# S5 in a four-layer trunk: the order of TensorE's work around the GELU's transposes

## The chip, the cores and the metric

The kernel runs on one core of a Trainium2 chip. The metric is the device time of one execution in microseconds (us). "Before" is the kernel as it was, "after" the one with the change. The engines are called as in the profile: PE is TensorE (PEld its weight loads), DVE is VectorE, ACT is ScalarE, POOL is GpSimd and SP is SyncE, which issues most transfers here.

## What is computed

A trunk of four layers on 512 positions of 1024 channels. Each layer is `x += mixer(rmsnorm(x))`, then `x += ffn(rmsnorm(x))`. The mixers are S5, gated linear attention, differential attention and S5 again. The change touches only the two S5 mixers, which are cut here to what matters:

```python
for u_c in chunks(u):                      # 64 positions, 64 groups of 16 channels, 64 states each
    bu_re, bu_im = u_c @ bb_re, u_c @ bb_im
    s = associative_scan(complex_diagonal, (a, bu))     # s[t] = a s[t-1] + bu[t]
    s += p * carry
    y_c = s_re @ c_re - s_im @ c_im
y = y + d_skip * h
z = gelu(y)
a, b = split(z @ w_glu)
x = x + a * sigmoid(b)
```

## The kernel before, in words

Each S5 mixer is a pipeline over eight blocks of 128 channels (`s5_pipe`, L1542). Step kk of its loop (L1668) works on several blocks at once, each at another stage. For block kk there are, in order:

- `up` (L1571): PE turns the normed input into channels by time (tile "up"), ACT copies it to `room`.
- `products` (L1582): 8 matmuls (in the profile two instructions each, since they are of full fp32) of the block with its input operators `inm` into the PSUM tile "V".
- `states` (L1590), `scan` (L1600) and `turn` (L1604): DVE multiplies V by cosines and sines (`cs`), scans twice along time and turns the result back into four products `prods`, one per k.
- `outputs` (L1617), one step later: 20 matmuls into the tile "y". For each of four groups b there is one on the "map" (the part of y that comes from the inputs of the same piece, L1622) and four on the states (`prods`, L1624). ACT then takes the GELU (L1626).
- `turned` (L1638): PE transposes the GELU's result into the tile "zp", and ACT rounds it to the high half of `zT` (L1643). `rest` (L1645): DVE subtracts to get the low half (L1647).
- `glu` (L1649), one step later still: 12 matmuls of the GLU's gate half (four pieces of the positions, three for high and low halves: L448, L449, L450) into four accumulators that stay open over all blocks. Its weights come as `whl`, a high half cast by ACT (`high`, L420) and a low half made by DVE (`low`, L428).

The first mixer (`s5_first`) also computes its operators on the way: powers (Q on DVE, X on DVE and POOL, L1239 to L1241), the operators' transposes ("xps", L1386, copied to `inm` by ACT, L1409), rows for the map ("rps", L1352, sent through DRAM back to SBUF by L1368 and L1377), and the phases of `cs`: two PE groups ("rough", L1199, and "angle", L1207), a clip on DVE (L1212) and sines on ACT. These are hung into the loop by named hooks, such as `beside` (L1908). The second mixer (`s5_second`) has them computed earlier and spilled to DRAM; its operators come back by transfers from SP (L1964, L1971).

The order on every engine is the order in which this code is written: `hand_all` (L376) switches the scheduler off inside the loop. Every engine takes its queue strictly in order. The PSUM tiles "up", "y", "zp", "xps", "cps" and "rps" share two buffers (`tp`, L395), so each waits for the reader of the one before the last; V has two banks, the accumulators and the phases' tiles share four.

Before, the loop of a step on PE reads: outputs of block kk-1, operators' transposes (first mixer), `up` of block kk+2, the GELU's transposes of block kk-1, products of block kk+1, then the GLU of block kk-2.

Of the kernel before, what the change touches and what calls it, by code (L numbers as in the profile page):

```python
# [22 lines left out]
P = 128  # L23
D = 1024
SEQ = 512
NT = SEQ // P
KT = D // P
# [313 lines left out]
class Trunk:  # L341
# [1200 lines left out]
    def s5_pipe(self, L, hu, zT, natural, room, get, before=None, hooks=None, steps=None, left=None):  # L1542
# [6 lines left out]
        mm = nc.tensor.matmul  # L1549
# [67 lines left out]
        def outputs(kk):  # L1617

            U, om, mop, q = room[kk % 4], get(kk, "out"), get(kk, "map"), hold[kk % 2][1]
            yb = self.tp("y")  # L1620
            for b in range(4):
                mm(yb[:, b], U[:, bs(b)], mop[:, bs(b)], start=True, stop=False)  # L1622
                for j in range(4):
                    mm(yb[:, b], q[:, j, b], om[:, j // 2, bs(b)], start=False, stop=j == 3)  # L1624
            z = room[4 + kk % 2].rearrange("p (t n) -> p t n", t=4)
            nc.scalar.activation(  # L1626
                z.rearrange("p t (g h) -> p g t h", h=16),
                yb[:].rearrange("p b (g t h) -> p (b g) t h", t=4, h=16), AF.Gelu_apprx_tanh,
            )
# [16 lines left out]
            d = dst(kk)  # L1646
            v.tensor_tensor(d[1], src(kk), d[0].bitcast(F32), op=ALU.subtract)  # L1647

        def glu(kk):  # L1649
            if not accs:  # L1650
                accs.extend(self.acc() for _ in range(NT))
            hl = hls[kk // 2]
            for t in range(NT):
                ts = slice(t * P, (t + 1) * P)
                self.mm3(
                    accs[t][:], zT[:, 0, kk, ts], zT[:, 1, kk, ts], hl[:, 0, kk % 2], hl[:, 1, kk % 2],
                    kk == 0, kk == KT - 1,
                )

        if hooks:  # L1660
            hook = lambda name, kk: hooks[name](kk) if name in hooks else None
            early = hooks.get("early", ())
            self.hand_all()
            if left:
                for kk in range(4):
                    up_first(kk)
            before(up, products)
            for kk in range(10):  # L1668
                if kk % 2 == 0 and kk:
                    hls[kk // 2 - 1] = self.high(stage[kk // 2 - 1], 2, 512)  # L1670
                hook("first", kk)
                if kk < 8:
                    states(kk)
                if kk == 7:
                    rest(5)
                hook("ahead of low", kk)
                if kk % 2 == 0 and kk:
                    self.low(hls[kk // 2 - 1], stage[kk // 2 - 1])
                hook("behind states", kk)
                if 1 <= kk < 9:  # L1680
                    outputs(kk - 1)
                hook("operators", kk)
                late = left and kk + 2 < 4
                if kk + 2 < 8 and not late:
                    up(kk + 2)
                hook("ahead of zp", kk)
                if 1 <= kk < 9:
                    turned(kk - 1)
                hook("behind zp", kk)
                if kk == 8:  # L1690
                    glu(6)
                if kk + 1 < 8:
                    products(kk + 1)
                hook("behind products", kk)
                if kk < 8:
                    scan(kk, 0)
                    scan(kk, 1)
                    hook("behind scans", kk)
                    for k in range(4):
                        turn(kk, k)  # L1700
                if late:
                    up(kk + 2)
                hook("ahead of rest", kk)
                if kk in early:
                    rest(kk - 1)
                hook("beside", kk)
                if 1 <= kk < 9 and kk != 6 and kk not in early:
                    rest(kk - 1)
                if kk % 2 == 0 and kk < 8:
                    stage[kk // 2] = self.staged(self.wb_src(wg, kk, D), 2, 512)  # L1710
                if kk >= 2 and kk != 8:
                    glu(kk - 2)
                hook("last", kk)
            self.hand()
            return accs
# [33 lines left out]
    def s5_first(self, ctx):  # L1749
# [5 lines left out]
        with self.tc.tile_pool(name="s5_0", bufs=1) as p:  # L1755
# [75 lines left out]
            def out_pads(kk):  # L1831
                self.s5_out_pads(oms[kk % 2], Q[kk // 2][0], slice(4 * (kk % 2), 4 * (kk % 2) + 4))
# [75 lines left out]
            def beside(kk):  # L1908
# [9 lines left out]
                if kk % 2 and kk < 7:  # L1918
                    Q[h + 1][2]()
                    Q[h + 1][3]()  # L1920
                    out_pads(kk + 1)
                if kk == 1:
                    phases((4, "clip"), (5, "clip"))

# [1 line left out]
            hooks = {  # L1926
                "first": first, "early": (2, 4), "ahead of low": ahead_of_low, "ahead of rest": ahead_of_rest, "operators": operators, "behind states": behind_states, "ahead of zp": ahead_of_zp, "behind zp": behind_zp,
                "behind products": behind_products, "behind scans": behind_scans, "beside": beside,
            }
            accs = self.s5_pipe(0, hu, zT, True, room, get, before, hooks)  # L1930
        self.x = self.xp.tile([P, NT, D], F32, tag="x", name="x")
# [875 lines left out]
```

## Time and profile before

| | us |
|---|---|
| median of three runs | 2251.64 |
| lowest and highest run | 2249.75, 2251.73 |
| the profiled execution | 2249.67 |
| span of its profile | 2248.0 |
| PE busy, share of the span | 2174.6, 97% |
| DVE busy, share of the span | 1635.6, 73% |
| first S5 pipeline, until its last GELU's transposes | 139.35 from the start |
| second S5 pipeline, from its first products to its last GELU's transposes | 1745.73 to 1829.43 |

The profile is that of one execution. A row of the timeline gives the start, the length, the engine, the line, the operation, output and inputs, the sizes and how many, and in brackets how long the engine had stood idle and what ended that. Lengths of matmuls are modelled: the next one starts before the length is over, so costs are better read from start to start. A row of the stretches gives the bounds, the length, then the busy time (and number of instructions) of PE, weight loads, DVE, ACT and POOL, the granted PE clock (1.00 is full), the share of the DMA engines and GB/s.

### The profile page before, as it was taken

What the parts mean: (1) busy time and instruction counts of PE and PEld (TensorE: products, weight loads), DVE (VectorE), ACT (ScalarE), POOL (GpSimd) and SP (SyncE); (2) the same over time, 40 slices, a digit from 0 to 9 for tenths busy, and PEclk for the clock granted to TensorE, in tenths of its full rate; (3) what the DMA queues carried; (4) which work ended last, traced back from release to release, by engine and by line L of the source; (5) the groups of instructions that cost most, each with busy time, mean ns of one, the idle gap of its engine ahead of it and who ended that gap; (6) DMA issues with size and microseconds to landing.
All of it is one profiled execution on the core that took longest, in us unless ns stands there. A gap on an engine that the chain in (4) does not pass through costs nothing.

```text
span 2248.0 us, 38450 instructions
## 1 busy us (share of the span) xinstructions
PE 2174.6 (97%) x15415; PEld 1971.6 (88%) x15415; DVE 1635.6 (73%) x2495; ACT 1138.7 (51%) x1827; POOL 341.1 (15%) x447
## 2 busy tenths in 40 slices
PE   6999999999999999999999999999999899999998
PEld 5888979989988899999888888999998888989997
DVE  9955868786878598776745676967766965957675
ACT  8534635444655365564435776644544234635443
POOL 5401141431211010100002221110000001101000
PEclk9999999999999999999999999999999999999999
DMA  4356666674863666765337465985631546766622
GB/s 90 65 171 169 164 159 174 174 184 131 206 152 95 168 168 191 179 171 139 104 128 160 96 148 141 243 207 136 184 94 47 160 141 159 196 160 164 165 76 75
DMA packets 309180, 333.62 MB, mean 148 GB/s; under 512 B 70477, under 2 KB 253033, under 8 KB 308874
## 3 DMA queue, kind: packets, MB, share of 16 engines
q1 hardware_dynamic: 238970, 238.93, 35.0%
q0 software_dynamic: 70032, 92.23, 21.9%
q8 instruction: 121, 1.98, 0.4%
q14 instruction: 57, 0.47, 0.1%
HBM read 297.16 MB, written 18.75 MB: 141 GB/s over the span
## 4 chain that ended last, share of the span: by engine, by line
PE 81%; DVE 8%; ACT 4%; issue 3%; DMA 1%; SPq 1%; POOL 0%; DVEq 0%; POOLq 0%; ACTq 0%
PE a L594 20%; PE acc L448 11%; PE acc L450 11%; PE acc L449 11%; PE c L594 10%; PE d L594 5%; PE y L1624 2%; DVE whl L428 2%; ACT whl L420 1%; PE op L2590 1%; PE V L1588 1%; PE s L2557 1%; PE tp L117 1%; PE acc L2645 1%; DMA wst<-in_ffn_w_down_dram 1%
## 5 line engine op out<-in xcount | busy, mean ns | idle before, releaser
L428 DVE TENSOR_TENSOR whl<-wst,whl 128x1024 fp32r<-128x1024 f32 x260 | 316.8, 1223 | 224.5 <-ACT whl L420 223.4
L420 ACT CAST whl<-wst 128x1024 fp32r<-128x1024 f32 x260 | 272.1, 1051 | 256.3 <-PE acc L450 164.6
L594 PE MATMUL a<-side,whl 128*128 128x256 f32 x3240 | 392.5, 277 | 6.7 <-DVE whl L428 6.3
L594 PEld LDWEIGHTS a<-side,whl 128*128 128x128 f32 x3240 | 379.0, 188 | 9.0 <-DVE whl L428 7.3
L448 PE MATMUL acc<-whl,act 128*128 128x512 f32 x704 | 276.2, 393 | 0.9 <-DVE g L768 0.9
L449 PE MATMUL acc<-whl,act 128*128 128x512 f32 x704 | 274.9, 391 | 0.0
L450 PE MATMUL acc<-whl,act 128*128 128x512 f32 x704 | 274.8, 390 | 0.0
L594 PE MATMUL c<-side,whl 128*128 128x256 f32 x2160 | 261.3, 277 | 3.5 <-DVE whl L428 3.5
L594 PEld LDWEIGHTS c<-side,whl 128*128 128x128 f32 x2160 | 253.0, 188 | 4.4 <-DVE whl L428 4.3
L428 DVE TENSOR_TENSOR whl<-slot,whl 128x1024 fp32r<-128x1024 f32 x105 | 127.6, 1221 | 60.7 <-ACT whl L420 60.7
L448 PEld LDWEIGHTS acc<-whl,act 128*128 128x128 f32 x704 | 132.4, 188 | 29.6 <-DVE g L768 1.5
L450 PEld LDWEIGHTS acc<-whl,act 128*128 128x128 f32 x704 | 132.4, 188 | 27.7
L449 PEld LDWEIGHTS acc<-whl,act 128*128 128x128 f32 x704 | 132.5, 188 | 26.4 <-issue 0.2
L420 ACT CAST whl<-slot 128x1024 fp32r<-128x1024 f32 x105 | 109.9, 1053 | 86.3 <-PE acc L450 46.3
L594 PE MATMUL d<-sides,whl 128*128 128x256 f32 x1080 | 132.3, 278 | 2.5 <-ACT whl L420 2.5
L594 PE MATMUL a<-sides,whl 128*128 128x256 f32 x1080 | 132.6, 279 | 1.6 <-DVE whl L428 1.2
L594 PEld LDWEIGHTS d<-sides,whl 128*128 128x128 f32 x1080 | 127.9, 188 | 3.3 <-ACT whl L420 3.3
L594 PEld LDWEIGHTS a<-sides,whl 128*128 128x128 f32 x1080 | 128.2, 188 | 2.8 <-DVE whl L428 1.4
L428 DVE TENSOR_TENSOR whl<-halves,whl 128x1024 fp32r<-128x1024 f32 x87 | 105.8, 1221 | 30.7 <-ACT whl L420 30.4
L420 ACT CAST whl<-halves 128x1024 fp32r<-128x1024 f32 x87 | 91.0, 1051 | 70.6 <-DVE halves L817 26.0
L759 POOL DMA_DIRECT2D wst<-in_ffn_w_gate_up_dram x44 | 57.2, 1299 | 448.7 <-DMA wst<-in_ffn_w_gate_up_dram 144.5
L865 ACT CAST act<-r 128x512 fp32r<-128x512 f32 (+1 forms) x110 | 66.1, 642 | 106.0 <-DVE r L846 85.4
(496 smaller groups left out, 4068.6 us busy)
## 6 DMA issues: line engine op xcount, KB each, us to landing
wst<-in_ffn_w_gate_up_dram SPq DMA_DIRECT2D x88, 512.0 KB, 4.6
wst<-in_ffn_w_down_dram SPq DMA_DIRECT2D x88, 512.0 KB, 4.6
slot<-in_ffn_w_gate_up_dram SPq DMA_DIRECT2D x69, 512.0 KB, 6.2
wst<-in_ffn_w_gate_up_dram POOLq DMA_DIRECT2D x44, 512.0 KB, 6.1
halves<-in_ffn_w_gate_up_dram SPq DMA_DIRECT2D x42, 512.0 KB, 6.5
wst<-in_s_w_glu_dram SPq DMA_DIRECT2D x32, 512.0 KB, 4.9
wst<-in_diff_w_qkv_dram SPq DMA_DIRECT2D x24, 512.0 KB, 4.4
slot<-in_ffn_w_gate_up_dram POOLq DMA_DIRECT2D x18, 512.0 KB, 9.2
```

The source lines that it names most:

```text
L117: tr.nc.tensor.transpose(p[:, j], h[:, j * P : (j + 1) * P], tr.ident[:])
L420: self.last["high"] = self.nc.scalar.copy(hl[:, 0], w[:])
L428: self.last["low"] = self.nc.vector.tensor_tensor(hl[:, 1], w[:], hl[:, 0].bitcast(F32), op=ALU.subtract)
L448: mm(out, lh, rh, start=first, stop=False)
L449: mm(out, lh, rl, start=False, stop=False)
L450: self.last["mm"] = mm(out, ll, rh, start=False, stop=last)
L594: mm(o, *two, start=first and not (j or k or n), stop=k == 3 and n == 2, skip_group_check=True,)
L759: nc.gpsimd.dma_start(w[:], left.quarter(*plus, b), accum_op=ALU.add)
L865: self.last["act high"] = nc.scalar.copy(dst[:, 0, j], src[:, j])
L1588: mm(V[kk][z][:, bs(b)], inm[:, z, bs(b)], U[:, bs(b)], start=True, stop=True)
L1624: mm(yb[:, b], q[:, j, b], om[:, j // 2, bs(b)], start=False, stop=j == 3)
L2557: nc.tensor.matmul(ss[m][:], qs[:, m, ts], ks[:, m, z], start=z == 0, stop=z == 1)
```

## The change

Four moves, and nothing is added to or taken from the work:

1. The products of block kk+1 stand ahead of the GELU's transposes of block kk-1 instead of behind them (both mixers).
2. A first piece of the GLU of block kk-2 stands ahead of those products: two matmuls at steps 3 to 5 of the first mixer, none there in the second, four at steps 6 to 8 of both. To let it run early, the GLU's 12 matmuls of blocks 1 to 6 come in another order: first those of two positions' pieces that use only the weights' high half.
3. The outputs of block 0 are no longer group by group. In the first mixer come the 16 matmuls on the states, then the four on the map; in the second the four on the map, then the 16.
4. In step 1 of the first mixer the low half of block 0 (`rest`) stands ahead of the clips of phases 4 and 5 on DVE.

```diff
             yb = self.tp("y")
-            for b in range(4):
+            if kk == 0:
+                by_map = [(b, U[:, bs(b)], mop[:, bs(b)]) for b in range(4)]
+                by_state = [(b, q[:, j, b], om[:, j // 2, bs(b)]) for b in range(4) for j in range(4)]
+                whole = by_map + by_state if left else by_state + by_map
+                for n, (b, x, y) in enumerate(whole):
+                    mm(yb[:, b], x, y, start=n == 0, stop=n == 19, skip_group_check=True)
+            for b in range(4 if kk else 0):
                 mm(yb[:, b], U[:, bs(b)], mop[:, bs(b)], start=True, stop=False)
...
-        def glu(kk):
+        order = {}
+
+        def glu(kk, n=12):
+
             if not accs:
                 accs.extend(self.acc() for _ in range(NT))
+            if kk not in order:
+                split = [(t, n) for t in range(2) for n in (0, 2)] + [(0, 1), (1, 1)] if 0 < kk < KT - 1 else []
+                order[kk] = split + [(t, n) for t in range(len(split) // 3, NT) for n in range(3)]
             hl = hls[kk // 2]
-            for t in range(NT):
-                ts = slice(t * P, (t + 1) * P)
-                self.mm3(
-                    accs[t][:], zT[:, 0, kk, ts], zT[:, 1, kk, ts], hl[:, 0, kk % 2], hl[:, 1, kk % 2],
-                    kk == 0, kk == KT - 1,
+            for t, m in order[kk][:n]:
+                mm(
+                    accs[t][:], zT[:, m // 2, kk, t * P : (t + 1) * P], hl[:, m % 2, kk % 2],
+                    start=kk == 0 and m == 0, stop=kk == KT - 1 and m == 2,
                 )
+            del order[kk][:n]
...
                 hook("ahead of zp", kk)
+                if 3 <= kk < 9:
+                    glu(kk - 2, 4 if kk > 5 else 0 if left else 2)
+                if kk + 1 < 8:
+                    products(kk + 1)
                 if 1 <= kk < 9:
                     turned(kk - 1)
                 hook("behind zp", kk)
                 if kk == 8:
                     glu(6)
-                if kk + 1 < 8:
-                    products(kk + 1)
                 hook("behind products", kk)
...
                     out_pads(kk + 1)
+
+            def last(kk):
                 if kk == 1:
                     phases((4, "clip"), (5, "clip"))
```

The built programs show three places. The first is PE at step 4 of the first mixer. The names are the PSUM tile that is written and what it is made from: xps the operators' transposes, up the input, zp the GELU's transposes, V the products, acc the GLU, cps transposes for the next operators.

```order
 L1386 MATMUL xps<-ident,X 64x64 x16
 L1567 MATMUL up<-ident,scr_96 128x128 x4
-L1642 MATMUL zp<-ident,z_366 128x128 x4
+L1666 MATMUL acc<-whl,zT 128x512 x2
 L1588 MATMUL V<-room_365,inm_101 128x128 x8
+L1648 MATMUL zp<-ident,z_366 128x128 x4
 L1285 MATMUL cps<-ident,craw 64x128 x8
```

Two GLU matmuls and the products moved in front of the transposes. The second place is PE at step 2 of the second mixer, where y is the end of the outputs and acc the start of the GLU; first before, then after.

```order
L1624 MATMUL y<-out_17598,prods 128x128 x4
L1567 MATMUL up<-ident,hu 128x128 x4
L1642 MATMUL zp<-ident,room_17592 128x128 x4
L1588 MATMUL V<-room_17592,operators 128x128 x8
L448 MATMUL acc<-whl,zT 128x512
```
```order
L1630 MATMUL y<-out_17598,prods 128x128 x4
L1567 MATMUL up<-ident,hu 128x128 x4
L1588 MATMUL V<-room_17592,operators 128x128 x8
L1648 MATMUL zp<-ident,room_17592 128x128 x4
L1666 MATMUL acc<-whl,zT 128x512 x12
```

Here only the products and the transposes traded places. The third is DVE at the end of step 1 of the first mixer: Q and dq are the powers, zT the low half, cs the clips, mods the next states.

```order
 L1240 TENSOR_TENSOR dq<-Q,pw 128x512
 L1241 TENSOR_TENSOR Q<-Q,dq 128x8x64
+L1653 TENSOR_TENSOR zT<-zp,zT 128x512
 L1212 TENSOR_SCALAR cs<-angle 128x512
 L1212 TENSOR_SCALAR cs_368<-angle 128x512
-L1647 TENSOR_TENSOR zT<-zp,zT 128x512
 L1593 TENSOR_TENSOR mods<-V,cs_368 128x512
```

The low half passed the two clips. The order of ACT and POOL is the same. On SP one transfer moved: in the second mixer the gain of the following norm (L532) is issued ahead of operators of later steps instead of behind them.

1 line of the change is left out of this document (added).

## The prediction

> **What bounds the kernel now.** I first read the busy time by stretches, then the chain of work that ended last, then who waited for whom. The profiled execution took 2249.67 us, of which the span is 2248.0 (the page's first line); the other 1.67 lie around it. The runs shown have a median of 2251.64, so my sum, which is made against the profiled execution, lands about 2 us below what a median would show. The rows of the stretches give the length, then the busy time of PE, weight loads, DVE, ACT and POOL, and the clock.
>
> ```profile
> span 2248.0 us, 38450 instructions
> ```
> ```profile
> 60.00:80.00 20.00, 19.25 (x191) 17.49 (x193) 20.00 (x32) 12.87 (x22) 4.26 (x8) 1.00 0.41 83
> ...
> 1760.00:1780.00 20.00, 18.75 (x150) 17.47 (x150) 20.00 (x30) 6.16 (x11) 0.32 (x3) 1.00 0.53 146
> ```
>
> In both S5 stages DVE is busy all the time and PE nearly so. Busy time alone would say that DVE is the bound and that the change, which moves PE work, gains nothing. The chain says otherwise. Here are its pieces around 58 us (start, length, what):
>
> ```profile
> 56.82 1.39 DVE Q L1241
> 58.22 1.20 DVE cs L1212 x2
> 59.41 0.61 DVE zT L1647
> ...
> 60.07 0.49 PE y L1622 x2
> 60.56 0.89 PE y L1624 x8
> ```
>
> Up to 60.02 us the chain is DVE's (59.41 and 0.61); from 60.07 on it is PE's. So before 58 us time given to PE buys nothing, and behind 60 us every gap of PE counts. The gaps are in the list of waits of PE (total, how often, longest), the first stage ahead of the second:
>
> ```profile
> PE zp L1642 <- ACT inm L1409: 3.2, 5, 0.7
> PE y L1622 <- DMA scr<-rd: 2.9, 1, 2.9
> PE y L1622 <- DVE zT L1647: 1.1, 1, 1.1
> ...
> PE zp L1642 <- ACT gain L1626: 0.7, 1, 0.7
> ```
> ```profile
> PE zp L1642 <- ACT room L1626: 4.1, 8, 0.7
> PE y L1624 <- DVE prods L1615: 2.6, 1, 2.6
> ```
>
> Most are one thing: the GELU's transposes (zp) stand at the head of PE's queue and wait for an evacuation by ACT, while work that is ready stands behind them.
>
> **The change part by part.** No matmul, DMA or vector instruction is added or dropped; all terms are gaps that fill or open. I write kk for the steps of the pipeline.
>
> *Pieces of the GLU ahead, first stage.* Rows of PE at kk = 4, kk = 6 and kk = 8:
>
> ```profile
> 93.29 0.66 PE L1567 MATMUL up<-ident,scr 128*128 128x128 f32 x4
> 94.63 0.66 PE L1642 MATMUL zp<-ident,z 128*128 128x128 f32 x4 [0.69 <-ACT inm L1409]
> ...
> 120.71 2.05 PE L1588 MATMUL V<-room,inm 128*128 128x128 f32 x16 [0.68 <-ACT inm L1409]
> ```
> ```profile
> 137.54 1.06 PE L1624 MATMUL y<-scr,prods 128*128 128x128 f32 x8
> 139.35 0.66 PE L1642 MATMUL zp<-ident,z 128*128 128x128 f32 x4 [0.75 <-ACT z L1626]
> 139.76 0.48 PE L448 MATMUL acc<-whl,zT 128*128 128x512 f32 x1
> 140.08 0.39 PE L449 MATMUL acc<-whl,zT 128*128 128x512 f32 x1
> 140.30 0.39 PE L450 MATMUL acc<-whl,zT 128*128 128x512 f32 x1
> ```
>
> By starts, a GLU matmul costs 0.32 us as first of its group (139.76 to 140.08) and 0.22 to 0.23 behind that. At kk = 3, 4 and 5 two of them (0.54) go into a gap that is still there, since the next products wait for the same copies (inm) as the transposes did: 0.69 idle at kk = 4, about as much at the others. The later group is shorter by 2 x 0.23, so 3 x 0.46 = 1.4 us. At kk = 6 the products stay at 120.71 (the copies set them), four matmuls (0.9) go ahead, and the transposes, 0.4 long (139.35 to 139.76), now follow the products: 0.9 - 0.4 = 0.5. At kk = 7 and 8 the outputs' last eight instructions end their issue 0.89 behind their start (the chain's rows of eight), at 138.43, and the transposes start at 139.35: a hole of 0.92, which four matmuls (0.32 + 3 x 0.22 = 0.98) fill. They save 4 x 0.23 less the 0.06 of overrun: 0.85 each, 1.7 together. At kk = 1 and 2 there is no piece, and products and transposes only trade places: nothing. Sum of the first stage: **3.6 us**.
>
> *Products ahead, second stage.* Here the products wait for no copy of ACT (their operators come by DMA):
>
> ```profile
> 1778.29 0.60 PE L1567 MATMUL up<-ident,hu 128*128 128x128 f32 x4
> 1779.20 0.66 PE L1642 MATMUL zp<-ident,room 128*128 128x128 f32 x4 [0.31 <-ACT room L1626]
> 1779.70 1.95 PE L1588 MATMUL V<-room,operators 128*128 128x128 f32 x16
> ```
>
> Four transposes take 0.50 to the next start (1779.20 to 1779.70), and from up to zp it is 0.91, so products that follow up at once start 0.41 sooner, and the GELU ends behind them. kk = 3, 4 and 5: 1.2 us. kk = 6, 7 and 8 have the four matmuls in a hole of the 0.7 kind, as above: 3 x 0.85 = 2.6. Sum: **3.8 us**. At kk = 1 and 2 the same trade is worth nothing, since DVE is late there:
>
> ```profile
> 1762.74 1.27 DVE L1615 TENSOR_TENSOR prods<-mods,cs 128x508 f32<-128x508 f32 x2
> ...
> 1773.29 1.27 DVE L1615 TENSOR_TENSOR prods<-mods,cs 128x508 f32<-128x508 f32 x2
> 1773.83 1.27 PE L1624 MATMUL y<-out,prods 128*128 128x128 f32 x8
> ...
> 1782.11 1.27 DVE L1615 TENSOR_TENSOR prods<-mods,cs 128x508 f32<-128x508 f32 x2
> ```
> ```profile
> 1784.47 1.06 PE L1624 MATMUL y<-out,prods 128*128 128x128 f32 x8
> ```
>
> The outputs of step 2 run while DVE still makes their last product (to 1774.56): PE cannot come sooner. One step on, DVE ends at 1783.38 and PE needs the last of it some 0.7 behind 1784.47: 1.8 us of room, more than the 0.4 gained there. The first stage has room too; its last DVE row and the first output matmuls behind it, and a wait of DVE:
>
> ```profile
> 129.53 1.28 DVE L1615 TENSOR_TENSOR prods<-mods,cs 128x508 f32<-128x508 f32 x2
> ...
> 133.97 0.39 PE L1622 MATMUL y<-scr,room 128*128 128x128 f32 x2
> ```
> ```profile
> DVE mods L1593 <- PE V L1588: 1.7, 1, 1.7
> ```
>
> DVE ends at 130.81, 3.2 us ahead of PE, and it sheds the 1.7 us when the products of step 7 come sooner. Each gain fits under this floor, but none by much.
>
> *First outputs' map.* In the first stage 16 matmuls on the states run instead of waiting 2.9 us for the map's transfer. In the second, four on the map fill part of the 2.6 us. Both end sooner on PE, and both I cost at nothing: behind them PE waits for DVE anyway (the chain up to 60.02; DVE's products to 1764.01).
>
> *Rest ahead of two clips.* The chain has 1.20 us of clips between Q and the first low half, which releases the second outputs. They leave the chain: **1.2 us**. The clips are late then, but what reads them (the angles of step 6, behind some 4.5 us of outputs) is later still.
>
> *What this opens.* The chain of ACT and PE that follows the first outputs moves up, and PE is out of work before Q is ready:
>
> ```profile
> 48.78 1.28 ACT L1626 ACT_TABLE_LOAD   x1
> ...
> 53.51 1.17 ACT L1409 COPY inm<-xps 64x512 f32<-64x512 f32 x2 [1.90 <-PE xps L1386]
> ...
> 57.72 0.40 PE L1200 MATMUL rough<-counts,frow 128*128 128x512 f32 x1
> ```
>
> The GELU can start when its table is loaded (50.06), the copies about 0.6 behind it instead of at 53.51, so the last of the roughs moves from 57.72 to about 54.9. Then PE idles about 3.1 us, until Q ends at 58.21. A gap of 2.9 us did this in the trace (PE alone; the number behind its busy time is the clock):
>
> ```profile
> 44.00:44.50 0.50, 0.00 (x0) 0.87 0.28 27
> ...
> 45.00:45.50 0.50, 0.50 (x3) 0.50 0.60 66
> ...
> 47.50:48.00 0.50, 0.50 (x5) 0.72 0.81 311
> ```
>
> That is not the full clock from about 44.4 to 47.8, at half of it for 3.4 us. The same over the second outputs, from 58.9 to about 61.5, takes 1.3 us. The cost lies between 0 (the gap falls apart over two stretches of counting) and 1.7 (half of 3.4). I take 1.3, for the nearest row is a gap of the same length. It eats the 1.2.
>
> The Trainium skill, TensorE: Matmul & The Clock Gate, Part 1 on the HAM clock gate, says that the array drops to half clock after an idle window of about 3.4 us, and that the window runs freely. The trace agrees on 0.50 and 3.4 us; by the skill's rule the gap of 3.1 us would cost 1.7 or nothing by where the window falls, and my sum would be 0.4 lower or 1.3 higher.
>
> *SP's queue.* The gain of the next norm (512 KB) is issued two steps sooner in the second stage, ahead of operators of later steps. Bounds: nothing, and one transfer of that size on the path:
>
> ```profile
> wst<-in_s_w_glu_dram SPq DMA_DIRECT2D x32, 512.0 KB, 4.9
> ```
>
> I take nothing: PE's list names no wait for a transfer in that stage, and what is loaded there is used a step or more later.
>
> **Sum**: 3.6 + 3.8 + 1.2 - 1.3 = 7.3 us. From the profiled 2249.67 that is 2242.4, from the median 2244.3; I take **2243.2** between them.
>
> **The rivals.** *The clock stays up.* The mechanism is the free position of the gap against the counting stretch: then the 1.3 is not paid, the gain is 8.6 and the time 2242. For it: the gaps of 0.7 us between 60 and 80 us left the clock at 1.00, and a gap cut in two is no longer than two of those. Against: 2.9 us did not.
>
> *DVE takes half back.* The transposes now stand behind the products, so the high halves come up to 1.9 us later (the products' row), and DVE, strictly in order, has the low halves in its queue ahead of the next states. Half a microsecond at each of seven steps lifts the floor by 3.5: gain 3.7, time 2247. For it: rooms of 1 to 2 us. Against: in the first stage PE itself is sooner by then.
>
> *The gain does not arrive.* DVE, busy 20.00 of 20.00, is the true bound, and the gaps come back as waits of y for prods: 2250 to 2251.6.
>
> *Slower: the clock breaks again and again.* The place is PE's chain from 58.9 to 140 and from 1774 to 1830. Each half-clock spell there costs 1.7 us of PE; 5 of them eat the 7.3, 7 make it slower by over 0.2%: about 2256. It decides once gaps near 3 us appear inside the chain. Against it: none of PE's gaps behind 61 us is over 0.75 and the change shortens them.
>
> **How the numbers follow.** Forecast 45%, clock stays up 20%, DVE takes half back 20%, gain does not arrive 9%, slower 6%. The range 2239.5 to 2248.5 takes in the first three cases with the 2 us by which executions differ. A measurement of this kernel can tell about 0.2% (4.5 us, so 2247.1) from no change: faster 0.45 + 0.20 + half of the third case, 0.75; same 0.19; slower 0.06.
>
> **What would show it.** Right: the chain passes from DVE to PE near 58.9 instead of 60.07; the waits of zp for ACT fall from 3.2 + 1.4 and 4.1 us to under 2.5 in all; the DVE wait for the products of step 7 (1.7) is gone; the half clock stands near 58 to 61.5 instead of 44 to 48; the last zp of the stages starts some 3.5 to 5 us sooner each. Wrong: waits of y for prods, of DVE zT for ACT zT, or of acc for whl inside the stages; or DVE's instructions longer than before, beside POOL's.

## The result, and the profile after

The changed kernel takes 2245.27 us (median of 12 runs, 2241.62 to 2249.66) against 2252.06 of before (12 runs, 2249.75 to 2257.28): ratio 0.997, 95% interval 0.9961 to 0.9979, so **6.8 us faster**. In a second set of runs, beside the last experiments, it was 2244.19 against 2251.53: 0.9963, 0.9950 to 0.9975. The forecast was 2243.2. The total is right, in part by luck: the sum behind it holds in one mixer, and in the other less than half of it arrived.

The profiled execution took 2241.62 us. Its span (the twelve instructions fewer than before are semaphore events), and its chain of work around 58 us:

```profile
span 2239.9 us, 38438 instructions
```
```profile
56.84 1.40 DVE Q L1241
58.24 0.04 issue
58.29 1.10 PE rps L1352 x30
59.39 0.73 PE y L1628 x2
60.12 1.71 PE y L1630 x8
```

The chain passes from DVE to PE at 58.29 now, not at 60.07: the clips and the low half have left it (this chain merges rows a little otherwise than the timeline, which has the first output at 59.32). But the first eight output instructions take 1.71 us, where they took 0.89 before. The stretches give the reason (the number behind POOL's busy time is the clock; the gap first, then the outputs):

```profile
54.90:58.30 3.40, 0.65 (x6) 0.15 (x4) 3.37 (x4) 3.33 (x6) 3.32 (x4) 1.00 0.21 43
...
58.50:59.00 0.50, 0.50 (x27) 0.50 (x23) 0.50 (x2) 0.50 (x2) 0.50 (x2) 0.50 0.00 0
...
61.00:61.50 0.50, 0.50 (x4) 0.50 (x4) 0.50 (x2) 0.00 (x0) 0.00 (x0) 0.50 0.79 83
```

PE idled before Q was ready, and the half clock that stood at 44 to 48 us stands at 58 to 62. The list of PE's waits in the first mixer, now headed by

```profile
PE rps L1352 <- DVE Q L1241: 3.9, 2, 2.7
PE up L1567 <- ACT gain L1632: 1.6, 1, 1.6
PE acc L448 <- ACT gate L2034: 1.5, 1, 1.5
PE V L1588 <- ACT inm L1409: 1.3, 3, 0.7
```

has no wait of the GELU's transposes (zp) left, in either mixer. In their place stand two waits that were not there before, for Q and for the gates at the stage's end, and `up`'s wait for the GELU has grown from 0.2 to 1.6 us: with the first outputs sooner, PE is out of work there too, from 49.2 us on, a gap that the prediction did not foresee.

**Reading the two traces side by side.** One execution differs from the next by several us, because spells of half clock, 3.4 us long and worth up to 1.7 us each, fall elsewhere in each. So a stage is better read from where the same instruction starts in two traces. I matched the instructions of DVE and ACT in order; the table has the difference of start against the profile of before (median of the eleven nearest to the point; minus is sooner). "First mixer" is the difference at 165 us, "between" and "second mixer" are what is added up to 1735 and from there to 1870 us. The fifth column gives the times of the half clock in the first mixer, the last says whether a spell starts at the second mixer's entry. "Step n" is block n from here on: the outputs of step n are those of block n, which stand in the loop's step n+1.

| profile | first mixer | between | second mixer | half clock in 44 to 65 us | spell from 1738 to 1749 |
|---|---|---|---|---|---|
| changed | +0.16 | -3.96 | -4.35 | 58.4 to 61.8 | no |
| changed, again | -1.48 | -4.69 | -3.15 | 53.0 to 56.4 | yes |
| second mixer only | +0.10 | +1.06 | -4.32 | 46.0 to 49.4 | no |
| first mixer only | -1.40 | -2.21 | +1.30 | 52.6 to 56.0 | yes |
| gates first | -3.13 | +2.17 | -3.04 | 52.0 to 55.4 | yes |
| step 2 turned first | -1.67 | +0.64 | -3.17 | 58.2 to 61.6 | yes |
| both of these mends | -4.30 | +1.78 | -3.06 | 53.7 to 57.1 | yes |
| both, one gap filled | -3.76 | +2.65 | -3.24 | 52.8 to 56.2 | yes |
| both, no pieces | -0.34 | -5.08 | -2.55 | 53.5 to 56.9 | no |
| both, map first again | -4.51 | +1.50 | -4.28 | 45.2 to 48.6 | no |
| x later | -3.20 | -0.92 | -2.98 | 52.0 to 55.4 | yes |
| both, gaps filled | -3.53 | +1.01 | -3.22 | none | yes |
| both, low half behind clips | -1.67 | -2.86 | -4.34 | 57.5 to 64.3 | no |

The second mixer's change gives 4.3 us in all four profiles that have it whole and no spell at its entry (4.28 to 4.35), and 3.0 to 3.2 in the seven with one. The profile of before has no such spell, and the run of the first mixer only, whose second mixer is as before, has it (+1.30). In before and in the changed kernel alike PE is busy for only 1.16 us in the idlest 3.41 us of this entry, so the idle place that draws the spell was there before the change. The column "between" is work that none of these kernels touches, and it swings from -5.1 to +2.7. Most of that follows the spells on the way: none from 165 to 1735 us in the three profiles with -4.0 to -5.1, 3.4 us of half clock in the one with -2.86, 6.8 in before and in the two with +1.0 and +1.1, and 10.2 in all others (-2.2 to +2.7).

### The profile page after: what moved, and what is told of

Read it like the earlier page. It is cut to its first block, busy times and chain, and to the rows that moved or that the text cites. A ratio compares the mean times of both kernels' runs of the same rounds, so it can differ in the third digit from the quotient of the medians.

```text
span 2239.9 us, 38438 instructions
## 1 busy us (share of the span) xinstructions
PE 2171.3 (97%) x15415; PEld 1967.9 (88%) x15415; DVE 1635.7 (73%) x2495; ACT 1137.5 (51%) x1827; POOL 337.6 (15%) x447
## 4 chain that ended last, share of the span: by engine, by line
PE 80%; DVE 10%; ACT 4%; issue 3%; DMA 1%; SPq 1%; POOL 0%; DVEq 0%; POOLq 0%; ACTq 0%
PE a L594 20%; PE acc L448 11%; PE acc L450 11%; PE acc L449 11%; PE c L594 10%; PE d L594 5%; DVE whl L428 2%; PE y L1630 2%; PE acc L1666 2%; ACT whl L420 1%; PE op L2607 1%; PE s L2574 1%; PE tp L117 1%; PE V L1588 1%; PE acc L2662 1%
## 5 line engine op out<-in xcount | busy, mean ns | idle before, releaser
L759 POOL DMA_DIRECT2D wst<-in_ffn_w_gate_up_dram x44 | 57.1, 1299 | 449.2 <-DMA wst<-in_ffn_w_gate_up_dram 174.0
```

The costliest lines, as they stand in the source:

```text
L759: nc.gpsimd.dma_start(w[:], left.quarter(*plus, b), accum_op=ALU.add)
```

## The experiments

All are edits of the changed kernel. The ratio is to the runs of before on the same chip. Theory A, formed from the two profiles, was that the first mixer's gain dies at the end of its own stage, at the gates; theory D, that DVE is set back at step 2.

### The second mixer alone

```diff
-            if kk == 0:
+            new = kk == 0 and left
+            if new:
...
-                if kk + 1 < 8:
+                if kk + 1 < 8 and left:
                     products(kk + 1)
```

and likewise for the pieces, with the clips back in `beside`.

> The change in the second mixer alone; the first mixer is as before. The two profiles at hand, laid side by side by DVE's instructions, show the changed kernel level with before (0.0 to 0.2 us) from 160 to 280 us, and 4.3 us gained between 1740 and 1850. Theory A (the first mixer's gain dies at the end of its own stage): at 160 us nothing is gained, in the second stage 4.3 us, and the whole is 4.3 us faster than before (near 2247.8). The prediction's split: 3.8 faster than before, and 3.5 slower than the full change (near 2248.5). Theory C (the 3.8 us that lie between 280 and 1740 us in the two profiles belong to the first mixer's change, which shifts all that follows against the clock's counting): also some 4 us slower than the full change, with half-clock spells near 290 and 640 us still there.

Measured: 2246.0 against 2250.36, 0.9981 (0.9972 to 0.9989), so 4.3 us faster. The table has +0.10 and -4.32, as theory A says; both spells that theory C asks for, at 285 to 288 and 650 to 654, are still there. By time the prediction's 3.8 cannot be told from 4.3; by position it can.

### The first mixer alone

The same edit with `not left`.

> The change in the first mixer alone; the second mixer is as before. Theory A: the last GELU's transposes of the first stage start at 138.7 instead of 139.35 us, but the first value matmuls of the GLU at 145.45, as late as before (145.29), so the whole is within 0.5 us of before (2251.6 to 2252.1). The prediction's split: 3.5 us faster (near 2248.5). Theory C (the middle of the kernel gains by another position against the clock's counting): 2 to 4 us faster, with the gain between 280 and 1740 us.

Measured: 2248.61 against 2250.36, 0.9994 (0.9985 to 1.0003). The first value matmul stands at 143.90 where before has 145.29: 1.4 us, neither nothing nor 3.5. Theory A was too strict: in this execution the half clock fell at 52 to 56 us, ahead of PE's wait for Q, where it costs nothing. Theory C's gain of 2 to 4 us in the middle of the kernel came at its lower end at most (2.2 us in the table), with spells of half clock at 281, 647 and 1292 us; one profile does not decide it.

### The gates first

```diff
         hl = self.wp.tile([P, 2, a, n], F32R, tag="whl", name="whl", bufs=5)
-        with self.tc.issue_after(self.behind["silu"].ins) if self.behind else nullcontext():
+        late = getattr(self, "late", None)
+        if late:
+            late[0] -= 1
+        with self.tc.issue_after(late[1].ins) if late and late[0] < 0 else nullcontext(), self.tc.issue_after(self.behind["silu"].ins) if self.behind else nullcontext():
             self.last["high"] = self.nc.scalar.copy(hl[:, 0], w[:])
```

where `late` holds a count of two and the last gate: two casts of weights pass ahead of it, not three.

> The changed kernel, with one cast of weights put behind the four gates on ACT at the head of each GLU. In the changed kernel's first mixer that cast waits for its transfer to 143.86 us, the gates stand behind it on ACT, and PE waits 1.54 us for the first gate. Theory A (this wait swallows what the first stage gained): the first value matmul starts near 143.9 instead of 145.45, and the whole is 1.5 us faster than the changed kernel (near 2243.8). Rival (the weights themselves are late, so PE waits for the cast instead): the same time as the changed kernel, with a wait of acc for whl.

In the changed kernel ACT and PE stand so at the stage's end:

```profile
143.86 1.04 ACT L420 CAST whl<-wst 128x1024 fp32r<-128x1024 f32 x1 [2.00 <-DMA wst<-in_s_w_glu_dram]
144.81 2.05 ACT L2034 ACTIVATE gate<-acc 128x512 f32<-128x512 f32 x4
...
145.45 0.50 PE L448 MATMUL acc<-whl,zT 128*128 128x512 f32 x1 [1.54 <-ACT gate L2034]
```

The kernel before has the same three at 143.69, 144.65 and 145.29; there only the weight load waits for the gate, 0.26 us, and PE does not. So PE's last accumulators were done sooner, and the gates were not. With the gates first:

```profile
140.58 2.51 ACT L2037 ACTIVATE gate<-acc 128x512 f32<-128x512 f32 x4 [0.17 <-ACT whl L423]
...
142.29 0.39 PE L451 MATMUL acc<-whl,zT 128*128 128x512 f32 x1
```

PE does not wait at all, for the gates or for the weights, so the rival falls. Measured: 2243.54 against 2250.36, 0.9967 (0.9955 to 0.9978), and -3.13 in the first mixer where the run of the first mixer alone, with its half clock at the same place, has -1.40: **1.7 us** lay in this wait.

### Step 2 turned first

```diff
+                swap = left or kk != 2
-                if kk + 1 < 8:
+                if kk + 1 < 8 and swap:
                     products(kk + 1)
```

and the products of that step behind `turned` again.

> The changed kernel, with the GELU's transposes of step 2 of the first mixer ahead of the products again, as before the change. In the changed kernel DVE waits 1.83 us there for the high half that these transposes feed. Theory D (this wait sets DVE back for the whole first stage, and PE waits for DVE at step 3): DVE's low half at step 2 starts near 70.2 instead of 72.1, the outputs of step 3 start 1 to 1.5 us sooner than at 89.07, DVE's last products of the stage end near 130.8 instead of 131.5. What reaches the end is then set by the transfer of weights behind it: 0.2 to 1.5 us faster than the changed kernel. Rival (DVE is late for other reasons, beside POOL): the outputs of step 3 start at 89 as in the changed kernel, and nothing is gained.

Measured: 2243.84 against 2250.36, 0.9971 (0.9961 to 0.9981); -1.67 in the first mixer against +0.16 with the half clock at the same place: **1.8 us**. The outputs of step 3 start at 87.39 instead of 89.07. Theory D holds for the place; for the cause the rows say more. First DVE's wait at step 2 (for the high half of block 1), then DVE's products of step 3 in the changed kernel, with POOL's instruction beside them (rows of these two engines alone):

```profile
72.09 0.69 DVE L1653 TENSOR_TENSOR zT<-zp,zT 128x512 fp32r<-128x512 f32 x1 [1.83 <-ACT zT L1649]
...
79.13 0.67 DVE L1615 TENSOR_TENSOR prods<-mods,cs 128x508 f32<-128x508 f32 x1
...
79.31 1.08 POOL L1264 TENSOR_TENSOR bb<-bb,gain 128x256 f32<-128x256 f32 x1
79.71 1.22 DVE L1611 SCALAR_TENSOR_TENSOR prods<-mods,cs 128x508 f32<-128x508 f32 x1
80.85 1.69 DVE L1615 TENSOR_TENSOR prods<-mods,cs 128x508 f32<-128x508 f32 x2
...
88.33 0.68 DVE L1653 TENSOR_TENSOR zT<-zp,zT 128x512 fp32r<-128x512 f32 x1
```

The same rows of the kernel before:

```profile
77.21 0.66 DVE L1615 TENSOR_TENSOR prods<-mods,cs 128x508 f32<-128x508 f32 x1
77.79 0.67 DVE L1611 SCALAR_TENSOR_TENSOR prods<-mods,cs 128x508 f32<-128x508 f32 x1
78.39 1.27 DVE L1615 TENSOR_TENSOR prods<-mods,cs 128x508 f32<-128x508 f32 x2
...
78.86 2.59 POOL L1264 TENSOR_TENSOR bb<-bb,gain 128x256 f32<-128x256 f32 x1
...
84.41 0.68 DVE L1647 TENSOR_TENSOR zT<-zp,zT 128x512 fp32r<-128x512 f32 x1
```

From the first product to the low half behind Q, the same instructions take DVE 7.20 us before (77.21 to 84.41) and 9.20 in the changed kernel (79.13 to 88.33). Before, POOL is the one that is held up (2.59 instead of 1.08). So at step 3 DVE loses 2.0 us beside POOL. The wait of 1.83 us ahead of it takes the new order and the half clock together: with the old order and the half clock at the same place, in the run of this section, DVE does not wait there. And in the second profile of the changed kernel, whose half clock stands sooner, the new order alone gives

```profile
70.68 0.69 DVE L1653 TENSOR_TENSOR zT<-zp,zT 128x512 fp32r<-128x512 f32 x1 [0.27 <-ACT zT L1649]
```

and 0.26 in the three other runs with this order and the half clock at 52 to 56 us. DVE still needs 9.19 us for the stretch there (77.73 to 86.92). So at full clock the order of step 2 makes DVE late by little, 0.5 us at its first product of step 3, and most is lost beside POOL.

### Both mends

> The changed kernel with both mends: one cast of weights behind the gates, and the GELU's transposes of step 2 of the first mixer ahead of the products. Apart they gave, by DVE's instructions at 165 us against before, -3.13 us (gates; the half clock fell at 52 to 56 us) and -1.67 (step 2; half clock at 58 to 62), where the changed kernel has +0.16 (58 to 62) and the first mixer's change alone -1.40 (52 to 56). Theory A and D (two separate waits): the gains add, -3.4 at 165 us with the half clock at 58 to 62, up to -4.9 otherwise, and the whole is 8.5 to 9.5 us faster than before. Rival (the transfers of weights behind the stage are the next bound): no more than -3.1 at 165 us.

Measured: 2241.59 against 2250.78, **0.9960 (0.9946 to 0.9974)**, the lowest of all ratios here, though its interval overlaps that of the changed kernel. The first mixer gives -4.30, with the half clock at 54 to 58: the gains add, but -4.9 was too much; the rival (no more than -3.1) falls. On the median it is 9.2 us faster than before, where 8.5 to 9.5 was expected. DVE and POOL at step 3:

```profile
77.50 0.65 DVE L1618 TENSOR_TENSOR prods<-mods,cs 128x508 f32<-128x508 f32 x1
...
77.97 3.77 POOL L1267 TENSOR_TENSOR bb<-bb,gain 128x256 f32<-128x256 f32 x1
78.08 0.67 DVE L1614 SCALAR_TENSOR_TENSOR prods<-mods,cs 128x508 f32<-128x508 f32 x1
78.67 1.27 DVE L1618 TENSOR_TENSOR prods<-mods,cs 128x508 f32<-128x508 f32 x2
...
84.70 0.68 DVE L1656 TENSOR_TENSOR zT<-zp,zT 128x512 fp32r<-128x512 f32 x1
```

POOL starts 0.47 us behind DVE's first product here and 0.18 behind it in the changed kernel, and the loser changes: DVE needs 7.20 us again.

### One gap filled

```diff
+        for _ in range(fill):
+            self.nc.tensor.matmul(rp[:, 0], self.ident[:], self.ident[:], start=True, stop=True)
```

> As the kernel with both mends, with 8 products of the identity (16 instructions, about 1.8 us) on PE ahead of the rows' products of step 2 of the first mixer, where PE idles 2.75 us for Q in the changed kernel. They add work and change no result. Theory B (the prediction's: this gap makes the half clock of 58 to 62 us): it is gone there, the outputs of step 1 end near 63.5 us as in the run of the first mixer's change alone, not at 64.9; 0.7 us faster on the median than with both mends, since the spell fell there in only half of the profiles. Rival (DVE sets the pace up to step 3): the outputs of step 1 end sooner, those of step 3 start at 87.4 all the same, and nothing is gained.

Measured: 2243.75 against 2250.78, 0.9970 (0.9958 to 0.9981). The half clock fell at 52 to 56 us, so the gap was not put to the test: inconclusive.

### Without the pieces

```diff
-                if 3 <= kk < 9:
-                    glu(kk - 2, 4 if kk > 5 else 0 if left else 2)
```

> As the kernel with both mends, without the pieces of the GLU ahead: all twelve stand behind again, in the new order. By the prediction's terms 3.6 us are lost in the first mixer (3 x 0.46, 0.5, 2 x 0.85) and 2.2 in the second (2.6 less the 0.41 that products ahead give alone at step 6): 5.8 us slower than the kernel with both mends. In the changed kernel the first stage gained 3.1 us of them between the outputs of step 3 and the end. Rival (DVE's floor is near): half of it, some 3 us.

Measured: 2246.47 against 2250.78, 0.9986 (0.9978 to 0.9995); on the median 4.9 us slower than with both mends. By position the first mixer loses 3.96 (-0.34 against -4.30; forecast 3.6), the second 1.8 (-2.55 against -4.3; forecast 2.2): 5.8 together, the forecast's 5.8. The waits of zp are back in part (2.1 us in all, one of three shown), and V waits for the copies:

```profile
PE V L1591 <- ACT inm L1412: 3.5, 5, 1.3
...
PE zp L1651 <- ACT z L1635: 0.7, 1, 0.7
```

### The map first again

```diff
-            if kk == 0:
+            new = kk == 0 and left
+            if new:
...
-            for b in range(4 if kk else 0):
+            for b in range(0 if new else 4):
```

> As the kernel with both mends, with the first outputs of the first mixer group by group again, the map first, as before the change. The prediction costs that move at nothing. Theory B: the wait for the map's transfer to 44.9 us is back, the half clock falls to 44 to 48 us, PE's chain up to the roughs ends near 57.7 again, no gap opens ahead of the second outputs, and they run at full clock: 0 to 1.4 us faster than the kernel with both mends. Rival (the move gains on ACT's and DVE's side): slower by some of the 2.9 us of the wait.

Measured: 2242.23 against 2250.78, 0.9969 (0.9957 to 0.9980), 0.6 us from both mends, within their scatter. The wait for the map's transfer is back (2.4 us), the half clock stands at 45.2 to 48.6, and the first mixer gives -4.51 against -4.30. The move is worth nothing that shows, as costed.

### x later

```diff
-        nc.gpsimd.dma_start(self.x[:], i["x"][0].rearrange("(t p) c -> p t c", p=P))
...
+                    if L == 0:
+                        with self.tc.issue_after(self.gated.ins):
+                            nc.scalar.dma_start(self.x[:], self.i["x"][0].rearrange("(t p) c -> p t c", p=P))
```

Here `gated` is the last of the four gates.

> The changed kernel, with the transfer of x (2 MB, for the residual, read some 25 us later) issued by ACT behind the four gates of the first mixer instead of by POOL as soon as DVE's last products are done (131.8 us). Theory A, in full: the weights that the third cast waits for until 143.86 us share the DMA engines with x, and this transfer, not PE, sets when the gates can run. Then the cast waits less, the gates run as the accumulators end, PE's wait of 1.54 us is gone, and the run is as fast as with the gates ahead of the cast: 1.2 to 1.7 us faster than the changed kernel. Rival (the weights come late because their buffer is free late, whatever else is moved): the cast still waits until about 143.9 us, and the time is that of the changed kernel.

ACT and PE at the stage's end, to be held against the rows of the gates above:

```profile
138.34 2.95 ACT L420 CAST whl<-wst 128x1024 fp32r<-128x1024 f32 x3
141.18 1.57 ACT L2033 ACTIVATE gate<-acc 128x512 f32<-128x512 f32 x3
...
142.23 0.39 PE L448 MATMUL acc<-whl,zT 128*128 128x512 f32 x1
```

The third cast no longer waits; the three run in one piece. Measured: 2244.36 against 2251.53, 0.9968 (0.9955 to 0.9980), by time no different from the changed kernel; by position -3.20 against -1.48 of the changed kernel's second profile, the half clock at the same place: 1.7 us, as much as the gates first. So the late gates are the work of x's 2 MB beside the weights.

### Both gaps filled

```diff
+                if kk == 1 and not left:
+                    V[2] = [self.sbank("V"), self.sbank("V")]
+                    for _ in range(6):
+                        mm(V[2][0][:, :P], self.ident[:], self.ident[:], start=True, stop=True)
```

on top of the filled gap of above.

> As the kernel with both mends, with 6 products of the identity on PE behind the operators' transposes of step 1 of the first mixer (a gap of 1.6 us from 49.2) and 8 more ahead of the rows' products of step 2 (the gap of 2.75 us). With the second gap alone filled, the half clock fell at 52 to 56 us, as in other runs, and 58 to 62 stayed untested. Theory B (the gaps make the spell): no half clock between 48 and 62 us, the outputs of step 1 end near 63.5. A spell at 52 to 56 costs nothing (PE waits for Q behind it), one at 58 to 62 costs 1.4 us at the outputs of step 1; so the median gains 0 to 0.7 over the kernel with both mends. Rival: the spell comes all the same, between the fillers.

Measured: 2244.10 against 2251.53, 0.9963 (0.9950 to 0.9977). The clock, at the place where it broke in the profiles without the map's wait:

```profile
50.00:52.00 2.00, 1.97 (x28) 1.71 (x23) 2.00 (x3) 1.97 (x4) 1.92 (x4) 1.00 0.01 4
52.00:54.00 2.00, 1.56 (x12) 1.33 (x13) 1.97 (x4) 1.62 (x3) 1.92 (x3) 1.00 0.00 0
...
58.00:60.00 2.00, 1.78 (x40) 1.41 (x39) 2.00 (x4) 1.97 (x4) 2.00 (x3) 1.00 0.00 0
60.00:62.00 2.00, 2.00 (x20) 2.00 (x19) 2.00 (x4) 0.34 (x1) 1.25 (x3) 1.00 0.58 94
```

No spell, as theory B says: this is the only one of the fourteen profiles without one from 44 to 65 us. PE is busy here for at least 2.9 of any 3.41 us between 40 and 65 us, where the other thirteen have a stretch with 1.65 or less ahead of the spell (more on that in the last section), so the gaps make it. Nothing is gained, though: -3.53 in the first mixer against -4.30.

### The low half behind the clips

```diff
                     out_pads(kk + 1)
-
-            def last(kk):
                 if kk == 1:
                     phases((4, "clip"), (5, "clip"))
```

> As the kernel with both mends, with the first low half of the first mixer behind the two clips again, as before the change. By the prediction's term the second outputs start 1.2 us later (near 60.1 instead of 58.9 to 59.3), and all behind them: 1.2 us slower than the kernel with both mends. Rival (DVE's floor at step 3 decides, and DVE does the same work in both orders): the outputs of step 1 start later, those of step 3 as before, and nothing is lost.

Measured: 2244.76 against 2251.53, 0.9966 (0.9953 to 0.9978). The second outputs start at 59.98 with

```profile
59.98 0.79 PE L1631 MATMUL y<-scr,room 128*128 128x128 f32 x2 [0.70 <-DVE zT L1656]
```

The run of step 2 turned first, whose half clock starts 0.7 us later, has 59.24 there, and 87.39 for the outputs of step 3 where this one has 89.10. So 0.74 us are lost at the second outputs and 1.7 at step 3, on either side of the forecast 1.2. But the half clock lasts twice as long here, to 64.3 instead of 61.6 us. That this is the work of the longer pause, and not of where the spell began, is not shown by one profile. The rival, nothing lost at step 3, is not borne out.

### The changed kernel again

> The changed kernel itself again, for a second profile and for times on the same chip as these runs. In its first profile nothing is gained at 165 us, with the half clock at 58 to 62 us, and 3.8 us between 280 and 1740 us. Theory E (the clock's spells fall where they like from one execution to the next): at 165 us between 0 and -1.5 us, by where the spell falls; in the second stage -4.3 us if no spell stands at 1742 to 1748 us, else -3.0; between 280 and 1740 us anything from -4 to +4. Rival (the gain between 280 and 1740 us belongs to the change): -3.8 us there again.

Measured: 2244.19 against 2251.53, as told at the top. The first mixer gives -1.48, with the half clock at 52 to 57, and the second -3.15 with a spell at its entry: theory E. In the middle the kernel gained 4.7 us, a little more than theory E allows and the rival's reading. Both profiles of the changed kernel have no spell there, which is most of that gain. The run of the first mixer alone has the same order of instructions up to there, and gained 2.2 with three spells on the way. Whether the changed kernel falls into those spells less often is **not settled**.

## Why the prediction was right, and where it was not

**The bound.** Right: DVE until 58 us, PE behind. That chain had been read for the two stages as a whole, though, and DVE turned out to be the bound once more, at step 3 of the first mixer.

**Products and pieces ahead, second mixer: forecast 3.8, measured 4.3.** The rows of before and of the changed kernel, each from the stage's first products to its last GELU's transposes:

```profile
1745.73 2.02 PE L1588 MATMUL V<-room,operators 128*128 128x128 f32 x16 [1.13 <-DVE room L1576]
...
1829.43 0.66 PE L1642 MATMUL zp<-ident,room 128*128 128x128 f32 x4 [0.75 <-ACT room L1626]
```
```profile
1741.93 2.02 PE L1588 MATMUL V<-room,operators 128*128 128x128 f32 x16 [1.13 <-DVE room L1576]
...
1822.22 0.64 PE L1648 MATMUL zp<-ident,room 128*128 128x128 f32 x4
```

That is 83.70 against 80.29 us, 3.41 less, and four matmuls of the GLU (0.9) are already done at the end: 4.3. Step by step, from the starts of the outputs, kk = 1, 2 and 3 give 0.55 together (1.23 won, 0.79 lost and 0.11 won; forecast nothing, nothing and 0.41), kk = 4 and 5 give 0.52 each (forecast 0.41), kk = 6, 7 and 8 give 0.93, 0.92 and 0.87 (forecast 0.85). The floor under it held: PE's list has one wait for DVE's products, at the first outputs, shorter than the 2.6 us of before:

```profile
PE y L1626 <- DVE prods L1615: 1.9, 1, 1.9
```

**First mixer: forecast 3.6 + 1.2 - 1.3 = 3.5, measured 0 to 1.5.** The starts of the first output matmul of each step (block), of the last transposes and of the first value matmul of the GLU, and their differences to before:

| | before | changed | changed, again | both mends |
|---|---|---|---|---|
| step 1 | 60.07 | -0.75 | -1.02 | -0.90 |
| step 2 | 74.80 | +0.49 | -0.92 | -0.87 |
| step 3 | 87.55 | +1.52 | +0.11 | -1.28 |
| step 4 | 100.89 | +1.16 | -0.25 | -1.51 |
| step 5 | 113.63 | +0.72 | -0.67 | -1.92 |
| step 6 | 125.36 | +0.24 | -1.15 | -2.38 |
| step 7 | 133.97 | -0.66 | -2.03 | -3.28 |
| last transposes | 139.35 | -0.64 | -2.01 | -3.27 |
| value half | 145.29 | +0.16 | -1.50 | -4.16 |

*The sizes were right, or nearly.* From step 3 to the end the second profile gains 0.36, 0.42, 0.48, 0.88 and, with the four matmuls that are already done, 0.88: 3.0, where the forecast has 3.1 for these steps. Of the 1.2 of the clips 0.75 to 1.02 is there at step 1: PE now makes the rows from Q (58.40 to 59.02 in the run of the first mixer alone) ahead of these outputs.

*The half clock was right in kind, and a matter of chance.* In the first profile it stands at 58 to 62 as forecast, and costs 1.6: the second outputs' rows and matmuls take 6.67 us (58.29 to 64.96) against 5.11 (58.40 to 63.51) in the run of the first mixer alone. In most others it falls at 52 to 57 instead and costs nothing, since the slowed work fills the gap ahead of Q, which is 0.59 us in the second profile and was 2.75 in the first (forecast 3.1):

```profile
58.43 0.68 PE L1352 MATMUL rps<-Q,bpad 128*32 128x64 f32 x30 [0.59 <-DVE Q L1241]
```

The price is then that of the rival "the clock stays up", by another mechanism than the one told: the clock does break, at the unforeseen gap of 1.6 us ahead of `up`.

*The step that failed* is the sentence "Each gain fits under this floor, but none by much". I read the floor of the first mixer from its last products alone (3.2 us of room there), and gave DVE's instructions at step 3 their old lengths. DVE lost 2.0 us beside POOL at step 3 in all five profiles with the changed order of step 2, which the prediction named only in its last line, and it came there late by its wait for the high half (0.27 us, and 1.83 where the half clock stood on PE's work ahead), the rival "DVE takes half back" at one step instead of seven. PE then waited 1.16 us for Q, in both profiles of the changed kernel:

```profile
88.46 0.68 PE L1352 MATMUL rps<-Q,bpad 128*32 128x64 f32 x30 [1.16 <-DVE Q L1241]
```

*What the prediction left out* is the end of the stage. It summed up to the last transposes and took what stands behind them as given; there, the gates are queued on ACT behind a cast that waits for a transfer, and 1.4 to 1.7 us of what had been gained were given back. One mark that it named had failed already ahead of that: the last transposes of the first mixer start 0.64 and 2.01 us sooner, not 3.5 to 5.

*The account closes* in the second profile, where the half clock costs nothing. Without it the forecast is 1.2 + 3.6 = 4.8. The clips gave 0.3 less by step 2, step 3 lost 1.0 instead of winning 0.46, and the later steps gave 0.1 less. That leaves 2.9, which is there at the last matmul of the gate half (142.15 against 145.06). The gates then take 1.4, and 1.5 is left. In the first profile the half clock takes another 1.4 and nothing is left.

**Why the total still fits.** The stages sum to 4.3 + 0 to 1.5 = 4.3 to 5.8 us, less than 7.3; the medians say 6.8 (4.7 to 8.8). The difference lies within the interval of the medians, and the rest of the kernel swings by as much. So the forecast of 2243.2 was met in part by luck: the first mixer gave 2 to 3.7 us less than its terms, the second 0.5 more, and the rest comes from outside both. The profiled pair's 8.1 holds 4.0 us from between the mixers, which no term of the prediction explains.

The other marks that came: the waits of zp are gone (forecast: under 2.5 us), DVE's 1.7 us for the products of step 7 too, and the gain's transfer on SP costs nothing that shows. The gain of the rival "DVE takes half back" is 3.8 by the prediction's own terms (7.3 less 3.5), not 3.7.

## What to carry to other kernels

Follow a gain to the next wait behind the stage that it was made in: here an in-order engine with one cast that waits for a transfer gave back what eight steps had saved. Where the change shifts one engine against another, look for instructions that are only fast because the other one happened to come later (DVE and POOL here). Where executions differ by more than the effect, compare starts of the same instruction stage by stage, beside profiles whose clock broke at the same place.

## What the runs showed of the hardware

- **Whether DVE or POOL is held up hangs on when POOL comes.** In the five profiles with the changed order at step 2, POOL's instruction starts 0.17 or 0.18 us behind DVE's first product and takes 1.07 or 1.08, and DVE's next takes 1.21 or 1.22 instead of 0.67. In the nine others POOL starts 0.47 us or more behind it and takes 2.29 to 3.77, and DVE's next keeps 0.67 to 0.69. The Trainium skill, SBUF — State Buffer, section "SBUF: two separate sides", calls the port pair that the two share an exclusive lock, held for a whole instruction by whoever starts first. The rows agree in that one of the two is held up while the other keeps its pace. But DVE's first product has started ahead of POOL in all fourteen, so the recorded starts do not tell the two cases apart by who was first. The moment of POOL's start was not moved by itself in any run.
- **The half clock is decided in stretches of 3.41 us that run on through the execution, and a stretch need not be idle as a whole.** Every spell but the one at the kernel's end lasts 3.41 or 6.83 us, and within a profile the spells start whole multiples of 3.413 us apart (53.00, 1739.19 and 1749.43 in the second profile of the changed kernel: 494 and 3 of them); from one execution to the next this grid lies elsewhere. Read on its grid, from 40 to 65 us, each profile but the one with the gaps filled has a stretch in which PE is busy for 0.63 to 1.65 us, with half clock right behind it, and no stretch at full clock with 1.79 or more is followed by one. The changed kernel's first and second profile show how the same gaps break the clock at one place or the other:

```profile
48.12:51.54 3.42, 1.79 (x37) 1.41 (x36) 3.42 (x5) 3.38 (x6) 3.26 (x5) 1.00 0.18 68
...
54.95:58.36 3.41, 0.66 (x8) 0.21 (x10) 3.38 (x4) 3.34 (x6) 3.33 (x4) 1.00 0.21 43
58.36:61.77 3.41, 3.41 (x41) 3.24 (x42) 3.41 (x7) 0.77 (x2) 2.43 (x4) 0.50 0.41 62
```
```profile
49.59:53.00 3.41, 1.41 (x19) 1.03 (x15) 3.41 (x5) 3.36 (x5) 3.33 (x5) 1.00 0.00 0
53.00:56.41 3.41, 3.41 (x18) 3.41 (x17) 3.38 (x4) 0.13 (x1) 3.32 (x4) 0.50 0.11 23
```

  So where a spell falls is chance from one execution to the next, but only among the places that are idle enough. Further on in the kernel the line is less sharp: stretches with 1.56 us left the clock full, and some with 1.94 did not; nor did one filled with matmuls of 128x2, at 645 us in before. Lengths of matmuls are modelled, so these busy times are too. The rule told in the prediction speaks of an idle window; the rows show a partly busy one, and they decide. The Trainium skill, TensorE: Matmul & The Clock Gate, Part 1, has the window run freely, and the profiles agree.
